# Second feed-forward product of a two-layer encoder: from plain row blocks to four phases, eight of 11 row pairs by seven products of quarters

## The chip, the cores and the metric

One NeuronCore of a Trainium2 chip runs the whole program. The metric is the device time of one execution in microseconds; three runs of the kernel before give 1254.53, 1255.04 and 1256.59 us, median 1255.04. One further execution was profiled, and every row below is from it.

## What is computed

Two layers over x of 512 tokens by 1024, float32. Each layer has four mixers and then the feed-forward part, which the change is about:

```python
h = rmsnorm(x, ffn_norm_pre[l])
gate, up = jnp.split(h @ ffn_w_in[l], 2, axis=-1)
f = (jax.nn.silu(gate) * up) @ ffn_w_out[l]
x = x + rmsnorm(f, ffn_norm_post[l])
```

`ffn_w_in` is 1024 x 5632 and `ffn_w_out` 2816 x 1024. The first line's product is called the first product here, the one with `ffn_w_out` the second. The output is x after the second layer.

## The kernel before, in words

**Numbers.** Every float32 factor is split in two: `hi` is the value rounded to fp32r by ScalarE (ACT), `lo` is the rest, by VectorE (DVE) or GpSimd (POOL). `mm3` multiplies by three passes of TensorE (PE), hi x hi, hi x lo and lo x hi.

**Order of the work.** The program is written by a planner at build time (`Builder.go`). Threads are Python generators that yield the engine of their next piece ("P", "A", "V", "G" for POOL, "D" for the SP queue) or a condition. `Timed` prices each instruction, `LAT` each handover, and `go` always takes the piece that can start earliest, ties by priority. The order on each engine is fixed by that; on the chip semaphores alone decide when each instruction starts. Plain loads are issued on SP (`dma`, L383), loads that add to a tile on POOL (`add_load`, L504; `sums` is the DVE part). Tokens stand for memory: 74 tiles "m" of 128x512 float32, 4 pairs "w" for split weights, 8 PSUM banks (3 "d", 5 "x").

**First product** (`ffn_in`). Three of the 22 blocks of gate and up are done plainly (`parts`), 19 by Strassen's seven products of quarters (`prod`, 256 columns wide). Their results are kept unsplit; 19 threads `f_conv` split them after the first product has ended (`self.conv`), and `ffn_act` does so at once for the first three.

**Second product** (`ffn_out`). For each 512-column half of the output and each of the 22 row blocks k, one weight block of 128x512 is split (`w_split`, on DVE or POOL) and four token blocks t are multiplied with it, 12 matmuls of 512 columns:

```python
for half in range(2):
    for k in range(KF):
        w = yield from self.w_get()
        for t in range(NT):
            self.mm3(b[half][t], (f[k][0][:, ts], f[k][1][:, ts]), w, k == 0, k == KF - 1)
```

In the second half the last eight row blocks are held back (`TAIL`) and done token block by token block, 24 matmuls each, so that the norm of block t (`chain`: square, `rstd` with a power on POOL, update of x, and the next layer's `pre_norm` with its transposes on PE) runs beside the matmuls of block t + 1. The next layer's first product starts on tokens 0 to 255 as soon as two blocks are normalised (`CUTS`). After layer 2, `put` stores x.

## Time and profile before

| | us |
|---|---|
| median of three runs | 1255.04 |
| the profiled execution | 1254.46 |
| its span | 1252.7 |
| second product, layer 1 | 505.4 to 625 |
| second product, layer 2 | 1125.8 to 1246.2 |

The span is from the first to the last instruction; 1.8 us of the execution lie around it. Engines are busy at the same time, so their times do not add up. PEld is PE's weight load, which overlaps its matmuls. In the chain, a piece is the work that released the next one. A line number L191 is that of a helper through which nearly all instructions are issued, so instructions are told apart by their tiles: `wh` and `wl` are hi and lo of a weight, `m` any tile, `bd` and `bx` PSUM banks, `in_wf` the feed-forward weights in memory.

### The profile page before, as it was taken

Reading aid. Unit: us, or ns where it says so; the run is one execution under the profiler, and the core shown is the slowest. Engines: PE = TensorE matmul, PEld = TensorE weight load, DVE = VectorE, ACT = ScalarE, POOL = GpSimd, SP = SyncE. Lnnn points to the kernel's source line nnn. Section 1 sums busy time; section 2 is a strip of 40 time slices with the busy share of each in tenths; the row PEclk is TensorE's granted clock in tenths of the full one; section 3 lists DMA queues with packets and bytes.
Section 4 is the critical chain, followed back from the end, with each engine's and each line's share of the span. In section 5 each row is a group of like instructions: output and inputs, shape, how many; then the busy total and the mean of one; then the engine's idle time right before and its main releaser. Section 6 shows DMA issues by size and latency. Waiting matters only on the chain.

```text
span 1252.7 us, 21225 instructions
## 1 busy us (share of the span) xinstructions
PE 1218.5 (97%) x7906; PEld 1067.7 (85%) x7906; DVE 783.7 (63%) x1602; ACT 658.2 (53%) x1448; POOL 232.6 (19%) x216
## 2 busy tenths in 40 slices
PE   7999999999999999999989899999999999999997
PEld 6876777789999999888887677677899999998886
DVE  6467674589667777612554766655897677765232
ACT  6476754565455555523438647445655455554330
POOL 5021111132111111212230111112411211102120
PEclk9999999999999999999989899999999999999999
DMA  6523125117776562325451221260386865532331
GB/s 216 196 89 97 48 60 179 68 62 178 172 189 179 149 152 77 116 87 167 155 195 51 68 85 35 77 204 24 91 192 164 196 165 147 144 99 96 102 117 68
DMA packets 77239, 155.11 MB, mean 124 GB/s; under 512 B 9040, under 2 KB 9424, under 8 KB 77136
## 3 DMA queue, kind: packets, MB, share of 16 engines
q1 hardware_dynamic: 65904, 133.31, 32.5%
q0 software_dynamic: 10944, 19.93, 9.8%
q8 instruction: 62, 1.02, 0.3%
q10 hardware_dynamic: 288, 0.52, 0.1%
q14 instruction: 41, 0.34, 0.1%
HBM read 147.44 MB, written 4.19 MB: 121 GB/s over the span
## 4 chain that ended last, share of the span: by engine, by line
PE 84%; DVE 6%; ACT 5%; issue 2%; POOL 1%; DMA 1%; SPq 0%; POOLq 0%; DVEq 0%; ACTq 0%
PE bx L191 42%; PE bd L191 41%; DVE m L191 5%; ACT m L191 4%; POOL s L191 1%; ACT L191 1%; DVE s L191 1%; DMA ws<-in_w 0%; ACT wh L191 0%; POOL wl L191 0%; POOL m L191 0%; DMA m<-in_w 0%; PE warm L191 0%; DVE wl L191 0%; DVE sbd L191 0%
## 5 line engine op out<-in xcount | busy, mean ns | idle before, releaser
L191 PE MATMUL bd<-m,wh 128*128 128x256 f32 (+1 forms) x1696 | 374.5, 315 | 1.1 <-DVE m L191 1.0
L191 DVE TENSOR_TENSOR wl<-m,wh 128x512 fp32r<-128x512 f32 x286 | 198.2, 694 | 155.1 <-ACT wh L191 145.5
L191 PEld LDWEIGHTS bd<-m,wh 128*128 128x128 f32 x1696 | 275.0, 191 | 22.6 <-issue 6.0
L191 ACT CAST wh<-m 128x512 fp32r<-128x512 f32 x318 | 196.9, 619 | 146.1 <-PE bd L191 74.2
L191 PE MATMUL bx<-m,m 128*128 128x256 f32 (+8 forms) x1736 | 255.8, 335 | 9.5 <-DVE m L191 9.0
L191 PE MATMUL bd<-m,wl 128*128 128x256 f32 (+1 forms) x848 | 264.3, 312 | 0.0
L191 PEld LDWEIGHTS bx<-m,m 128*128 128x128 f32 (+3 forms) x1736 | 195.5, 178 | 59.2 <-issue 26.0
L191 DVE TENSOR_TENSOR m<-m,m 128x512 f32<-128x512 f32 (+3 forms) x286 | 172.9, 622 | 42.0 <-ACT m L191 40.2
L191 PEld LDWEIGHTS bd<-m,wl 128*128 128x128 f32 x848 | 161.8, 191 | 9.3
L191 PE MATMUL bx<-wh,m 128*128 128x512 f32 x472 | 163.7, 392 | 0.0
L191 PE MATMUL bx<-m,wh 128*128 128x256 f32 x832 | 154.3, 283 | 0.9 <-ACT bd L191 0.9
L191 PEld LDWEIGHTS bx<-m,wh 128*128 128x128 f32 x832 | 129.8, 192 | 1.3 <-ACT bd L191 1.3
L191 PE MATMUL bd<-wh,m 128*128 128x512 f32 x360 | 128.8, 392 | 0.0
L506 POOL DMA_DIRECT2D m<-in_wf x76 | 67.1, 976 | 315.5 <-DVE m L191 87.3
L191 ACT CAST wh<-ws 128x512 fp32r<-128x512 f32 x86 | 53.3, 621 | 126.2 <-PE bd L191 76.9
L191 DVE TENSOR_TENSOR wl<-ws,wh 128x512 fp32r<-128x512 f32 x56 | 42.2, 754 | 122.5 <-ACT wh L191 122.0
L191 PE MATMUL bx<-m,wl 128*128 128x256 f32 x416 | 117.7, 283 | 0.0
L191 PEld LDWEIGHTS bx<-wh,m 128*128 128x128 f32 x472 | 89.1, 189 | 19.0 <-issue 0.5
L191 POOL TENSOR_TENSOR wl<-m,wh 128x512 fp32r<-128x512 f32 x32 | 49.1, 1535 | 286.4 <-ACT wh L191 236.1
L191 POOL TENSOR_TENSOR wl<-ws,wh 128x512 fp32r<-128x512 f32 x30 | 47.9, 1596 | 263.9 <-ACT wh L191 242.8
L191 PE MATMUL bd<-m,m 128*128 128x256 f32 (+1 forms) x624 | 92.4, 303 | 0.9 <-ACT m L191 0.9
L191 PE MATMUL bx<-wl,m 128*128 128x512 f32 x236 | 92.3, 391 | 0.0
(105 smaller groups left out, 1479.6 us busy)
## 6 DMA issues: line engine op xcount, KB each, us to landing
m<-in_wf SPq DMA_DIRECT2D x234, 256.0 KB, 3.8
m<-in_wf POOLq DMA_DIRECT2D x76, 256.0 KB, 4.9
ws<-in_wf SPq DMA_DIRECT2D x34, 512.0 KB, 3.6
m<-in_w SPq DMA_DIRECT2D x64, 256.0 KB, 4.5
ws<-in_w SPq DMA_DIRECT2D x16, 512.0 KB, 3.8
m<-in_wo SPq DMA_DIRECT2D x24, 256.0 KB, 3.8
m<-in_x SPq DMA_DIRECT2D x14, 256.0 KB, 4.8
m<-in_rpb SPq DMA_DIRECT2D x12, 256.0 KB, 5.1
```

Of the source, the lines that this page charges most:

```text
L191: return f(out, *a, **k)
L506: self.nc.gpsimd.dma_start(q[name], src, accum_op=ALU.add)
```

## The change

The 22 row blocks become 11 pairs j. A pair's activations are four quarters (tokens 0 to 255 and 256 to 511 by row block 2j and 2j + 1: A11, A12, A21, A22), its weights four blocks of 128x512 (B11, B12, B21, B22). Eight pairs use Strassen's seven products with Winograd's sums, three pairs (`std`, and D11, D21) the eight plain ones. The sums of products are collected over all pairs, so there are four phases: A collects A11 B11 in bank 1 and s5 t1 in bank 2; B adds s6 t2 in bank 3, A12 B21 in bank 1, s4 B22 in bank 2, and the three plain pairs (with bank 4); C adds s3 t3 and D adds A22 t4 in bank 3. A "bank" here is two PSUM banks, one for each 128-token block u.

The activations' sums s3 to s6 are made in place on DVE (`f_pair`), each factor is split as it is needed (`f_factor`, 256 wide). The weights' sums are made by loads that add: t1, t2 and t4 follow from B11 in one tile (`t_chain`), each added after the one before has been split; t3 is a plain load and one that adds. `w_factor` splits a weight, up to LOOK = 8 steps ahead of its use, always on DVE. Loads start up to 14 steps ahead (WAHEAD), activations are split up to seven ahead (FAHEAD). Between phases `out_joins` forms the sums of banks that the results need, and PE waits for them where a bank is used again (`before`). Tokens 0 to 255 are complete after phase B and go through `half`, `finish` and, between layers, `pre_norm` while PE is in C and D; tokens 256 to 511 after C (one column half) and D (the other), where the last two products of the phase are done token block by token block.

```diff
+WAHEAD = 14
+HKEEP = 8
+LPRI = 1.5
+LOOK = 8
+FAHEAD = 7
+KP = KF // 2
+KS = KP - 3
...
 def stream(self):
-            for h in range(2):
-                for i in range(KF // 2):
-                    yield d["wf2"][l, h, i], "m" if h and 2 * i >= KF - TAIL else "w"
+            yield l, "out"
...
+    def out_factors(self, l, n):
...
+        std = lambda j: [("B", j, "B11", ((1, "A11"),)), ("B", j, "B21", ((1, "A12"),)),
+                         ("B", j, "m12", ((2, "A11"), (4, "A21"))), ("B", j, "m22", ((2, "A12"), (4, "A22")))]
+        steps = []
+        for j in range(KS):
+            steps += [("A", j, "B11", ((1, "A11"),)), ("A", j, "t1", ((2, "s5"),))]
+        done = KS
+        for j in range(KS):
+            steps += [("B", j, "t2", ((3, "s6"),)), ("B", j, "B21", ((1, "A12"),)), ("B", j, "B22", ((2, "s4"),))]
+            while done < KP and (done - KS + 1) * KS <= (j + 1) * (KP - KS):
+                steps += std(done)
+                done += 1
+        steps += [("C", j, "t3", ((3, "s3"),)) for j in range(KS)]
+        for j in range(KS):
+            steps += [("D", j, "t4", ((3, "A22"),))]
+        for j in range(KS, KP):
+            steps += [("D", j, "D11", ((3, "A21"),)), ("D", j, "D21", ((3, "A22"),))]
...
+        for j in range(KP):
+            q = lambda h, k: w[l, h, j][:, k * 512:(k + 1) * 512]
+            if j < KS:
+                self.spawn(self.t_chain(o[j], at[j, "B11"], {x: at[j, x] for x in ("t1", "t2", "t4")},
+                                        (q(0, 0), q(1, 0), q(1, 1), q(0, 1))), 0)
+                parts = (("B21", (q(0, 1),)), ("B22", (q(1, 1),)), ("t3", (q(1, 0), q(1, 1))))
+            else:
+                parts = (("B11", (q(0, 0),)), ("B21", (q(0, 1),)), ("m12", (q(1, 0),)), ("m22", (q(1, 1),)),
+                         ("D11", (q(0, 0),)), ("D21", (q(0, 1),)))
+            for x, p in parts:
+                self.spawn(self.w_part(o[j], x, at[j, x], p), 0)
...
+    def t_chain(self, o, at, use, src):
+        yield lambda: at < self.wuse + WAHEAD and len(self.tok["m"]) >= 1 + ROOM
...
+        self.dma(t, src[0], 262144)
...
+        for more, before, name in zip(src[1:], ("B11", "t1", "t2"), ("t1", "t2", "t4")):
+            yield lambda: before + ".s" in o["n"]
+            yield from self.more_load(t, more, use[name])
+            o["n"].add(name)
...
+    def more_load(self, tile, src, use):
+        self.cur.pri = use / 1000.0 - 5.0
+        yield "G"
+        self.nc.gpsimd.dma_start(tile, src, accum_op=ALU.add)
+        self.cost += 1000.0
+        self.moved = max(self.moved, self.start + self.cost + 650.0) + 262144 / 180.0
+        self.cur.after = self.moved + 1500.0
...
+    def w_factor(self, i, o, x):
+        yield lambda: x in o["n"] and (
+            self.wnext == i and (self.tok["w"] or len(self.tok["m"]) >= 2 + FROOM)
+            or self.wnext >= self.out_at and i < self.wuse + LOOK and len(self.tok["m"]) >= 4 + FROOM)
...
+            yield from self.split(w[:2], o[x], "V")
...
+    def f_pair(self, j, f, o):
...
+        yield "V"
+        tt(a[:, hi], b[:, hi], a[:, hi], ALU.subtract)
+        n |= {"fA11", "fs5", "fA12", "fA22"}
+        yield lambda: "fA11.s" in n
...
+        tt(a[:, lo], a[:, lo], a[:, hi], ALU.add)
...
+        tt(b[:, lo], a[:, lo], b[:, lo], ALU.subtract)
...
+        tt(a[:, hi], a[:, lo], b[:, hi], ALU.subtract)
...
+    def f_factor(self, i, o, x):
+        yield lambda: (self.fnext == i and "f" + x in o["n"] and i < self.fuse + FAHEAD
+                       and len(self.tok["m"]) >= 1)
...
+        yield "A"
+        self.act.activation(t[:, 0:HALF], src, AF.Copy, scale=-1.0 if x == "s6" else 1.0)
+        yield "V"
...
+            self.dve.tensor_tensor(t[:, HALF:L], src, t[:, 0:HALF].bitcast(F32), ALU.subtract)
...
-    def f_conv(self, i, a, f):
...
 def ffn_in(self, l, h, ok, f):
+        for j in range(KP):
+            self.outs[l][j] = {"n": set()}
+            self.spawn(self.f_pair(j, f, self.outs[l][j]), 3)
...
 def ffn_act(self, i, b, f):
-        self.dve.tensor_tensor(a, a, b[1], ALU.mult)
+        self.dve.scalar_tensor_tensor(a, a, -1.0, b[1], ALU.mult, ALU.mult)
-        o = self.mr2()
-        yield from self.split(o, a)
...
+    def out_joins(self, x1, x2, x3, x4, n, g, acc, res):
+        def one(u):
...
+            yield lambda: "A" in n
+            yield "A"
+            self.act.copy(p, x1[u])
+            n.add(("p", u))
+            yield "V"
+            tt(r, p, x2[u], ALU.add)
+            n.add(("r", u))
+            yield lambda: "6" in n
+            yield "V"
+            tt(v, p, x3[u], ALU.add)
+            n.add(("v", u))
+            yield lambda: "B" in n
+            self.spawn(self.half(u, 0, x1[u], "d", g, acc[u], res), LPRI)
+            yield "V"
+            tt(v, v, x2[u], ALU.add)
+            self.give("x")
+            self.spawn(self.half(u, 1, v, None, g, acc[u], res), LPRI)
+            if KS < KP:
+                yield "V"
+                tt(r, r, x4[u], ALU.add)
+                self.give("dx"[u])
+            yield lambda: ("C", u) in n
+            yield "V"
+            tt(r, r, x3[u], ALU.add)
+            n.add(("c", u))
+            self.spawn(self.half(2 + u, 1, r, None, g, acc[2 + u], res), u - NT)
+            yield lambda: ("D", u) in n
+            yield "V"
+            tt(p, p, x3[u], ALU.add)
+            self.give("x")
+            self.spawn(self.half(2 + u, 0, p, None, g, acc[2 + u], res), u - NT)
...
 def ffn_out(self, l, g, gi, h, ok, f):
+        before = {("B", 1): "p", ("B", 2): "r", ("C", 3): "v", ("D", 3): "c"}
...
+            tail = mine[-2:] if ph in "CD" else []
...
+                for us in ((0,), (1,)) if tail and i == mine[-1][0] else ((0, 1),):
+                    for i2, dst, j2, y2, w2, wl in rest:
+                        t = held[j2, y2]
+                        for u in us:
+                            if (ph, dst) in before:
+                                yield lambda: (before[ph, dst], u) in n
+                            yield "P"
+                            self.mm3(bank[dst][u], (t[:, u * P:(u + 1) * P], t[:, HALF + u * P:HALF + (u + 1) * P]), w2,
+                                     dst in fresh, i2 == last[ph, dst], skip_group_check=True)
```

## Rows read from the trace of the kernel before

**Rows 1.** The page, busy time of the engines: us, share of the span, instructions
```profile
PE 1218.5 (97%) x7906; PEld 1067.7 (85%) x7906; DVE 783.7 (63%) x1602; ACT 658.2 (53%) x1448; POOL 232.6 (19%) x216
```

**Rows 2.** The page, chain that ended last, share by engine
```profile
PE 84%; DVE 6%; ACT 5%; issue 2%; POOL 1%; DMA 1%; SPq 0%; POOLq 0%; DVEq 0%; ACTq 0%
```

**Rows 3.** The chain in order of time, second product: start us, us, what
```profile
506.10 2.06 PE bx L191 x9
...
604.03 10.88 PE bd L191 x48
```

**Rows 4.** Stages: us; PE, PEld, DVE, ACT, POOL busy; granted clock; DMA share; GB/s
```profile
317.40:498.80 181.40, 181.40 (x1514) 181.40 (x1514) 131.63 (x232) 95.97 (x197) 26.32 (x31) 1.00 0.61 152
505.40:565.20 59.80, 59.80 (x268) 49.61 (x268) 25.17 (x38) 24.43 (x45) 12.57 (x6) 1.00 0.31 102
565.20:625.00 59.80, 59.80 (x274) 49.69 (x273) 25.18 (x50) 24.68 (x61) 13.36 (x13) 1.00 0.46 154
```

**Rows 5.** Timeline of DVE, runs back to back: start us, us, instruction, count
```profile
287.88 2.76 DVE L191 TENSOR_TENSOR m<-m 128x256 f32<-128x256 f32 x8
...
506.55 5.50 DVE L191 SCALAR_TENSOR_TENSOR m<-m,m 128x512 fp32r<-128x512 f32 x9
```

**Rows 6.** Timeline of ACT, a run back to back
```profile
505.48 3.24 ACT L191 ACTIVATE m<-m 128x512 fp32r<-128x512 f32 x6
```

**Rows 7.** The tile in_wf: ns min/median/max of each load's issue; landing of all
```profile
L384 SPq DMA_DIRECT2D m<-in_wf x234: 327/328/1524, 187.7 to 1206.1; - x117
L506 POOL DMA_DIRECT2D m<-in_wf x76: 862/875/1938, 283.5 to 1094.9; - x76
...
DMA to landing us min/median/max: 2.5/4.1/9.5
```

**Rows 8.** DMA queues, 280 to 317 us: packets, MB, share of 16 engines
```profile
q1 hardware_dynamic: 2691, 4.91, 41.4%
q0 software_dynamic: 1152, 2.10, 34.1%
```

**Rows 9.** DMA queues, 317 to 400 us
```profile
q1 hardware_dynamic: 5667, 10.30, 39.2%
q0 software_dynamic: 2350, 4.29, 32.3%
```

**Rows 10.** Adding loads, median us to landing: all, then 283.5 to 297 us
```profile
m<-in_wf POOLq DMA_DIRECT2D x76, 256.0 KB, 4.9
...
m<-in_wf POOLq DMA_DIRECT2D x5, 256.0 KB, 8.0
```

**Rows 11.** PE's waits, 495 to 506 us: us, times, longest
```profile
PE bd L191 <- DVE m L191: 0.5, 1, 0.5
```

**Rows 12.** PE's waits, 600 to 662 us
```profile
PE bx L191 <- DVE m L191: 3.1, 1, 3.1
```

**Rows 13.** Stage 630 to 645 us, columns as in rows 4
```profile
630.00:645.00 15.00, 11.85 (x78) 11.65 (x78) 11.76 (x25) 7.35 (x22) 6.32 (x8) 0.77 0.76 246
```

**Rows 14.** Timeline of PE, eight transposes at full clock
```profile
622.45 1.03 PE L191 MATMUL bx<-ident,m 128*128 128x128 f32 x8
```

**Rows 15.** The chain in order of time, after the wait of rows 12
```profile
638.78 1.97 PE bx L191 x8
640.75 2.56 PE bd L191 x12
643.31 9.29 PE bx L191 x72
652.60 8.64 PE bd L191 x72
```

**Rows 16.** Timeline, end of the last two token blocks
```profile
1240.82 0.60 ACT L191 ACTIVATE m<-bx 128x512 f32<-128x512 f32 x1 [4.75 <-PE bx L191]
...
1246.26 0.60 ACT L191 ACTIVATE m<-bx 128x512 f32<-128x512 f32 x1 [4.75 <-PE bx L191]
...
1248.47 0.74 DVE L191 SCALAR_TENSOR_TENSOR m<-m,s,m 128x512 f32<-128x512 f32 x1
```

More of the change, by code (lines that the diff above doesn't have):

```diff
@@ L446, in w_load @@
                 n += (7 if src[1] > NP else 4) + (3 if src[1] == KF - 1 else 0)
+                continue
+            if kind == "out":
+                n = self.out_factors(src, n)
                 continue
@@ new lines, in w_part @@
+    def w_part(self, o, x, at, parts):
+        yield lambda: at < self.wuse + WAHEAD and len(self.tok["m"]) >= 1 + ROOM
+        self.take("m", 1)
+        o[x] = self.m()
+        yield "D"
+        self.dma(o[x], parts[0], 262144)
+        if len(parts) > 1:
+            yield from self.more_load(o[x], parts[1], at)
+        else:
+            yield "V"
+        o["n"].add(x)
+    def more_load(self, tile, src, use):
[6 more added lines that the diff above has]
+        yield "V"
+        self.cost = 0.0
@@ new lines, in w_factor @@
+    def w_factor(self, i, o, x):
+        yield lambda: x in o["n"] and (
+            self.wnext == i and (self.tok["w"] or len(self.tok["m"]) >= 2 + FROOM)
+            or self.wnext >= self.out_at and i < self.wuse + LOOK and len(self.tok["m"]) >= 4 + FROOM)
+        early = self.wnext != i
+        self.taken.add(i)
+        while self.wnext in self.taken:
+            self.taken.remove(self.wnext)
+            self.wnext += 1
+        if self.tok["w"] and not early:
+            self.take("w")
+            w = (self.whp.tile([P, 512], F32R, tag="wh", name=self.nm("wh")),
+                 self.wlp.tile([P, 512], F32R, tag="wl", name=self.nm("wl")), "w", 1)
+        else:
+            self.take("m", 2)
+            w = (*self.mr2(), "m", 2)
+        if x[0] == "m":
+            yield "A"
+            self.act.activation(w[0], o[x], AF.Copy, scale=-1.0)
+            yield "V"
+            self.dve.scalar_tensor_tensor(w[1], o[x], -1.0, w[0].bitcast(F32), ALU.mult, ALU.subtract)
+        else:
+            yield from self.split(w[:2], o[x], "V")
+        o["n"].add(x + ".s")
+        if "t4" not in o or x in ("B21", "B22", "t3", "t4"):
+            self.give("m")
+        self.wrdy[i] = w
@@ L1513, in pair_sums @@
         self.give("d")
-        self.spawn(self.f_conv(i, a, f), 4)
-    def f_conv(self, i, a, f):
-        yield lambda: self.conv
-        yield from self.need(2, 0)
-        o = self.mr2()
-        yield "A"
-        self.act.activation(o[0], a, AF.Copy, scale=-1.0)
-        yield "V"
-        self.dve.scalar_tensor_tensor(o[1], a, -1.0, o[0].bitcast(F32), ALU.mult, ALU.subtract)
-        self.give("m")
-        f[i] = o
+        f[i] = a
     def ffn_in(self, l, h, ok, f):
@@ L1557, in ffn_in @@
                     who[4].add(n)
+                    if i + (who is new) >= KF:
+                        self.give("m", 4)
             old = new
-        self.conv = True
-        self.give("m", 28)
     def ffn_act(self, i, b, f):
-        yield from self.need(3, 0)
+        yield from self.need(1, 0)
         a = self.m()
@@ new lines, in ffn_act, with half, finish @@
+        f[i] = a
+    def half(self, t, i, y, bank, g, acc, res):
+        yield from self.square(acc, i, y)
+        yield "V"
+        j = self.att[t // 2][t % 2] if bank else y
+        if i == 0:
+            self.dve.scalar_tensor_tensor(j, y, -1.0, g[i], ALU.mult, ALU.mult)
+        else:
+            self.dve.tensor_tensor(j, y, g[i], ALU.mult)
+        if bank:
+            self.give(bank)
+        res[t, i] = j, not bank
+        if (t, 1 - i) in res:
+            res[t] = 1
+    def finish(self, t, gi, h, ok, acc, res):
+        yield lambda: t in res
+        r = yield from self.rstd(acc)
+        for i in range(2):
+            xs = self.x[t][i]
+            yield "V"
+            self.dve.scalar_tensor_tensor(xs, res[t, i][0], r, xs, ALU.mult, ALU.add)
+            if res[t, i][1]:
+                self.give("m")
+            if h is None:
+                self.spawn(self.put(t, i, xs), t - NT)
+        if h is not None:
+            yield lambda: "h" in res
+            yield from self.pre_norm(t, gi, h, ok, False)
@@ L1629, in dense @@
             f = {}
+            self.fnext, self.fuse = 0, 0
             yield from self.ffn_in(l, h, ok, f)
```

161 lines of the change are left out of this document (120 added, 41 removed).

## The prediction

> **What bounds the kernel now.** I read the page's table of busy time first. TensorE (PE) is busy for 1218.5 us, 97% of the span, VectorE (DVE) for 783.7 [rows 1]. A busy PE is not proof, so the chain that ended last comes next: PE holds 84% of it [rows 2]. In order of time the chain shows the second feed-forward product as an unbroken string of matmuls, nine in 2.06 us at its start and 48 in 10.88 us near its end, 226.7 ns each [rows 3]. The table by stage confirms it: in both halves of the product PE is busy for 59.8 of 59.8 us at full clock, while DVE works 25.2 us and the DMA engines 0.31 and 0.46 of the time [rows 4]. So in this stage time is matmuls counted, and there is room on every other engine. The first product (the first line of the same table) matters because it is already done by Strassen's seven products: its PE is busy for 181.4 of 181.4 us with DVE at 73% and the DMA engines at 0.61. That is the nearest evidence that such a scheme can feed PE.
>
> **The matmuls removed.** A quarter product is 6 matmuls of 512 columns (two token blocks, three passes), 6 x 226.7 ns = 1.36 us. A row pair takes 8 now and 7 by Strassen. Per layer that is 48 x 11 = 528 matmuls now and 42 x 8 + 48 x 3 = 480 after: 48 fewer, 10.88 us by the row of 48; over two layers **-21.76 us**, all on the path. Their shape does not change, so neither does their price.
>
> **Work on DVE and ScalarE (ACT).** Back to back, DVE gives a 512-wide instruction every 0.603 us ((5.50 - 0.68)/8) and a 256-wide one every 0.335 us [rows 5]; ACT a 512-wide one every 0.524 us ((3.24 - 0.62)/5, one alone lasting 0.62) [rows 6]. Per layer there are 8 x 7 + 3 x 6 = 74 weight factors to split (512 wide) and 8 x 7 + 3 x 4 = 68 activation factors (256 wide), each once on ACT and once on DVE; 32 sums of activations, 256 wide; 12 joins and 8 gain products, 512 wide, all on DVE. DVE: 74 x 0.603 + 68 x 0.335 + 32 x 0.335 + 20 x 0.603 = 90.2 us in 480 x 0.2267 = 108.8 us, 83% (now 42%). ACT: 142 x 0.524 = 74.4 us if its narrow instructions cost as much as the wide, and under 10 for squares and copies: 78% at most. The 19 conversions of `f_conv` and the three of `ffn_act` go. I cost all of this at nothing: PE covers it, as it covers 73% in the first product. If the cover were gone (PE waiting on something else) it would matter by phase: phase A asks per pair for 2 x 0.603 + 3 x 0.335 = 2.2 of 2.72 us, and phase C, with its joins and gain products, for 12.3 in 10.9 us. Up to eight weight factors and seven activation factors may be prepared ahead, 10.9 us of PE, so I expect C to live on stock.
>
> **Transfers.** SP: 50 plain loads a layer at 0.33 us each are 16.5 us of issue, no bound. POOL: 4 adding loads per Strassen pair, 32 a layer at 0.88 us, 28 us of issue [rows 7]; POOL's low halves in this stage go, and DVE's sum above holds them. On the engines, from 280 to 317 us the plain queue moved 4.91 MB (18.7 loads) in 41.4% of 37 us, 0.82 us a load, and the adding queue 2.10 MB (8 loads) in 34.1%, 1.58 us a load [rows 8]. Check: the first product's 5 plain and 2 adding loads per 10.08 us ask for 72%, and the engines show 39.2 + 32.3 = 71.5% [rows 9]. A Strassen pair now asks for 4 x 0.82 + 4 x 1.58 = 9.6 us against 9.52 us of PE; a plain pair for 4.9 against 10.9. Per layer 91.5 of 108.8 us: it fits, but phase A does not. There t1 and the next link, t2, are both released per pair: 0.82 + 2 x 1.58 = 4.0 us against 2.72 us, with phase B's plain loads beside it.
>
> **The chain in phase A** decides the size of the gain. t1 is B11 with another quarter added in place, so it needs: B11 split (1.4 us: 0.62 on ACT, 0.68 on DVE, a handover), an adding load, t1 split (1.4 us). B11 may be split eight steps before its own use, so 10.9 us are there. Issue to landing of an adding load has a median of 4.9 us, 8.0 us in a burst of them [rows 10], and 9.5 us is the longest of any weight load [rows 7]: chains of 7.7, 10.8 and 12.3 us. The first costs nothing, the last 1.4 us in every eight steps, 2.8 us for A's sixteen. With the queue asked for more than it can give I take the long row: 2.8 us a layer, **+5.6 us**. Bounds: 0, and everything in one line, 15 adding and 10 plain loads, 31.9 us, begun some three products (4.3 us) ahead of A: the last t1 is split at 29.0 us where it is due at 20.4, 8.6 us a layer, 17.2 in all.
> The Trainium skill (DMA: Bandwidth & Descriptors, section on the anatomy of one DMA on the gpsimd path) fits a load as 2.0 us plus bytes over 436 GB/s, an estimated 2.6 us here, and by that the chain would be 5.4 us and the sum 5.6 us lower; the trace's loads that add take longer than this fit, so I don't use it.
>
> **New waits of PE.** At A's end PE's third product waits for bank 1 copied and its fourth for a sum on DVE; they come 1.4 and 2.7 us later, about what ACT and DVE need. At C's end D's second token block waits one DVE instruction, 0.6 us and a handover, with three matmuls, 0.68 us, to cover it. Today's same kind of wait, PE on DVE at the end of the first product, is 0.5 us [rows 11]. I take 0.8 us a layer, **+1.6 us** (0 to 4). ACT's and DVE's next splits queue behind these; the stock covers that.
>
> **The layer's edge.** Today PE waits 3.1 us for the last token block's norm [rows 12], and the granted clock of 630 to 645 us is 0.77, a part of it at 1.2 instead of 2.4 GHz [rows 13]: eight transposes take 1.97 us, 1.03 us a little earlier [rows 14], and 12 matmuls 2.56 us where 1.44 would do at the 120 ns of the 72 in 8.64 us further on [rows 15]. That gap costs 3.1 + 2.7 = 5.8 us, the 0.65 us over in the 72 after it included. After the change two token blocks are normalised under C and D, so the next layer's first half starts at once; but the last two blocks' chains get longer and PE's order is fixed by the same planner with the same misjudgement. I take **0** (-5.8 to +3).
>
> **The end.** After the last matmul come a square, the power, two updates and the store [rows 16]. Now a join of 0.6 us and a handover go in front and the two last blocks follow each other by 1.4 us instead of 5.4, so their updates share DVE: **+1.0 us** (0.7 to 2.4).
>
> **Sum.** The profiled execution took 1254.46 us (span 1252.7; the median of the runs is 0.6 us higher). 1254.46 - 21.76 + 5.6 + 1.6 + 0 + 1.0 = **1240.9 us**, a 1.1% gain. With A's chain fully hidden and the edge's gap closed it would be 1229.5; with A's upper bound 1252.5.
>
> **Rivals.**
> *All hidden, and the edge closes*: 1229 to 1234 us. For it: the first product shows no wait, and today's gap stands exactly where the new order puts work. Against: the landings of [rows 10]. Chance 0.13.
> *The adding queue sets phase A's pace*: 5 to 8.6 us a layer, and where a wait grows to the 3 us of [rows 12] the clock falls for a few us more: 1246 to 1256 us, 1250 in the middle. For it: 4.0 us asked in 2.72. Against: t2 isn't due until B and B11 is loaded early. Chance 0.19.
> *POOL's queue blocks itself*: slower. POOL issues in program order, and the planner prices an adding load at 4.6 us (1.0 + 0.65 + 1.46 + 1.5 in the code). A t2 waiting at the head for its t1's split holds up the t1s behind it, for up to 4.9 + 1.4 = 6.3 us each time. Gain and other costs balance at (21.76 - 2.6)/2 = 9.6 us a layer, so it decides from two such holds a layer: 1254.46 - 21.76 + 4 x 6.3 + 2.6 = 1260.5 us. For it: real landings are later than priced [rows 10]. Against: in the first product the same queue waits for splits too, and PE is never idle [rows 4]. Chance 0.08.
> *The clock falls in phase A*: short waits between short bursts might keep PE at its lower level. The sixteen products would take twice 21.8 us: 1254.46 - 21.76 + 43.5 + 2.6 = 1278.8 us. The trace has half clock after the 3.1 us wait and full clock through the waits of 0.5 us. Chance 0.02.
> The Trainium skill (TensorE: Matmul & The Clock Gate, section on HAM oscillation) tells of such a loop, where waits for loads make every burst start slow; by that rule this rival's price holds, and the trace agrees only for the long wait.
>
> **How the numbers follow.** The forecast, 1234 to 1247 us, has 0.58. A measurement of this kernel can tell 0.2%, 2.5 us. Faster by more: 0.58 + 0.13 + three quarters of 0.19 = 0.85; within: 0.05; slower: 0.10. The range of 1231 to 1252 leaves out both slower rivals, the top of the queue's case and the best of the first, some 0.2.
>
> **What would show it.** Right: 226.7 ns per matmul with 480 a layer in the second product, a stage of 109 to 114 us instead of 119.7, DVE near 83% in it, the DMA engines near 0.9 in phase A, and PE's waits in it on a DVE split with an adding load before it. Wrong: unbroken matmuls in phase A (chain hidden); waits of 3 us or a granted clock under 1.0 in it; a POOL queue idle on a split while later t1 loads are due; waits in phase C on DVE (stock not built). The prediction falls if the matmuls' price changes or the stage isn't bound by PE at all.

## The result, and the profile after

The changed kernel takes **1245.9 us** (median of four runs, 1244.61 to 1246.83) where the kernel before takes 1254.88 on the same chip: a ratio of 0.9926, 95% interval 0.9912 to 0.9940. So it is faster by 9.0 us where 13.6 were forecast. The profiled execution took 1245.09 us, its span is 1243.3 us.

The page of the changed kernel: busy time, the chain that ended last, the two large DMA queues.

```profile
PE 1203.1 (97%) x7810; PEld 1050.1 (84%) x7810; DVE 883.8 (71%) x1867; ACT 707.5 (57%) x1604; POOL 246.7 (20%) x255
...
q1 hardware_dynamic: 72672, 136.46, 34.6%
q0 software_dynamic: 20160, 36.71, 17.8%
...
PE 76%; issue 7%; DVE 7%; DMA 4%; ACT 4%; POOL 2%; SPq 0%; POOLq 0%; DVEq 0%; ACTq 0%
```

Beside [rows 1, 2]: 96 matmuls fewer, 15 us less of busy PE, 100 us more of DVE, and the chain now spends 76% of the span on PE, not 84%. Which stages those detours are in, the table by stage shows: phase A of layer 1, phases B and C, phase D, the stage of [rows 13], and phase A of layer 2.

```profile
507.96:532.92 24.96, 23.26 (x98) 17.82 (x97) 21.22 (x45) 17.22 (x39) 12.33 (x15) 1.00 1.10 242
532.92:600.00 67.08, 67.08 (x297) 55.57 (x296) 52.75 (x111) 42.92 (x100) 12.03 (x14) 1.00 0.80 201
600.00:622.00 22.00, 21.90 (x105) 17.92 (x103) 17.66 (x43) 12.72 (x38) 5.20 (x7) 1.00 0.49 159
...
630.00:645.00 15.00, 13.00 (x95) 12.49 (x94) 10.78 (x27) 7.17 (x25) 4.38 (x7) 0.89 0.86 294
...
1121.30:1147.00 25.70, 23.79 (x98) 17.77 (x98) 21.19 (x45) 16.78 (x38) 12.45 (x15) 1.00 1.09 239
```

Phases B to D run as the first product did in [rows 4]: PE without a gap but for 0.4 us at the turn to D, though DVE is at 79% in B and C. Phase A alone is loose. It holds 96 matmuls, 21.76 us, and takes 24.96 and 25.70. The matmuls' price stands (chain in order of time, phase B, 226.7 ns each):

```profile
535.81 2.72 PE bx L198 x12
```

To set the two kernels beside each other I cut the span at four places in PE's timeline, in each layer: the first 256-wide matmul of the feed-forward part, the first 512-wide one (the second product begins), the last 512-wide one, and the next layer's first 256-wide one of that part (all of layer 2's mixing lies in that last stretch, the edge between the layers with it). Lengths in us, worked out from those starts (the second product with its last matmul, 0.23 us, which the last row holds as well in layer 2):

| stretch | before | after | difference |
|---|---|---|---|
| start to layer 1's feed-forward part | 284.78 | 285.31 | +0.53 |
| first product, layers 1 and 2 | 221.15, 221.15 | 222.65, 222.65 | +3.00 |
| second product, layers 1 and 2 | 121.48, 119.70 | 114.26, 113.17 | -13.75 |
| edge and mixing of layer 2 | 277.80 | 276.49 | -1.31 |
| last matmul's start to the end | 6.85 | 9.00 | +2.15 |
| span | 1252.7 | 1243.3 | -9.4 |

The first row says nothing of the change. Up to there PE does the same instructions in the same order in the kernel before, the changed kernel and every run below, and the stretch takes 284.2 to 287.5 us in their profiled executions. The mixing of layer 2, at the end of the fourth row, spreads too (227.3 to 229.3 us), so half a microsecond of that row is no finding either.

Four detours have to be explained: phase A, the end of the first product, the edge, the tail.

**Phase A.** PE's waits, 507 to 535 us (us, times, longest):

```profile
PE bx L198 <- DVE wl L198: 1.1, 3, 0.5
PE bx L198 <- ACT wh L198: 0.6, 2, 0.5
```

The DMA queues of the changed kernel, 500 to 530 us (packets, MB, share of 16 engines), and its weight loads (KB, median us to landing):

```profile
q0 software_dynamic: 2017, 3.69, 68.9%
q1 hardware_dynamic: 1812, 3.32, 34.2%
...
m<-in_wf POOLq DMA_DIRECT2D x17, 256.0 KB, 8.9
m<-in_wf SPq DMA_DIRECT2D x12, 256.0 KB, 7.2
```

PE waits for the split of a weight (`wl` and `wh` are its halves), each time in front of a t1 of the last pairs: the starts of its matmuls show gaps from 523.7 us on, the largest 0.74 (the view, which counts from the modelled end of a matmul, has 1.7 of the 3.2 us). Split late means landed late: 8.9 us against 4.9 in [rows 10]. The queues' shares add up to 103% of the engines.

**The first product.** The chain in order of time near its end (start us, us, what):

```profile
480.74 0.76 DVE m L198 x2
481.50 0.60 DVE wl L198
482.10 0.35 DVE m L198
482.44 0.39 ACT m L198
482.83 0.02 issue
482.86 0.44 DVE bd L198
483.30 0.04 issue
483.34 1.69 PE bd L198 x12
```

DVE's timeline at the same place:

```profile
481.08 0.42 DVE L198 TENSOR_TENSOR m<-m,m 128x256 fp32r<-128x256 f32 x1
481.41 0.69 DVE L198 TENSOR_TENSOR wl<-m,wh 128x512 fp32r<-128x512 f32 x1
482.01 0.76 DVE L198 TENSOR_TENSOR m<-m 128x256 f32<-128x256 f32 x2
482.86 0.43 DVE L198 TENSOR_TENSOR bd<-bd,m 128x256 f32<-128x256 f32 x1
```

The sum in the bank `bd` at 482.86 is one of the first product's own, and PE stands for it: one wait of 1.36 us by the matmuls' starts, at the same place in both layers and absent before. Ahead of it in DVE's order stand 256-wide instructions that touch no bank, a split (481.08) and two sums (482.01): by their shapes the new work on the activations. But they are over by 482.77, and the sum in the bank starts 0.03 us after the copy that it reads, which ACT ends at 482.83. So it is this copy that is late, and not for DVE's time. Copies from a bank to a tile or another bank in ACT's timeline:

```profile
462.02 0.36 ACT L198 COPY bd<-bx 128x256 f32<-128x256 f32 x1 [0.94 <-PE bx L198]
464.90 0.37 ACT L198 COPY m<-bx 128x256 f32<-128x256 f32 x1 [0.94 <-PE bx L198]
472.10 0.36 ACT L198 COPY bd<-bx 128x256 f32<-128x256 f32 x1 [0.62 <-PE bx L198]
482.17 0.36 ACT L198 COPY bd<-bx 128x256 f32<-128x256 f32 x1 [0.94 <-PE bx L198]
482.44 0.38 ACT L198 COPY m<-bx 128x256 f32<-128x256 f32 x1
```

Each block of the first product has two of them, one into a bank and 2.9 us later one into a tile. For the block that begins with 472.10 the second comes at 482.44, 7.5 us late, behind the first copy of the next block. In the code (`pair_first`) it asks for two free tiles "m" first. The plan, which is made at build time by the code shown, has none free for it at this block and the next in the changed kernel, e1, e5 and e8, which all show the wait, and three or more in the kernel before, e3, e6, e10 and e12, which do not. What e3, e6, e10 and e12 hold back are the sums and splits of activations; each split made ahead takes a tile. (The free tiles are read from the plans; no trace shows them.)

**The edge and the tail.** PE's one wait from 600 to 640 us:

```profile
PE bx L198 <- DVE m L198: 1.9, 1, 1.9
```

The transposes behind it, in PE's timeline:

```profile
634.37 3.53 PE L198 MATMUL bx<-ident,m 128*128 128x128 f32 x16 [1.91 <-DVE m L198]
```

The timeline of DVE, ACT and POOL behind the last matmul, which begins at 1234.3 us:

```profile
1234.74 0.69 DVE L198 TENSOR_TENSOR m<-m,bx 128x512 f32<-128x512 f32 x1 [0.67 <-PE bx L198]
1235.35 0.69 DVE L198 SCALAR_TENSOR_TENSOR m<-m,m 128x512 f32<-128x512 f32 x1
1235.46 0.63 ACT L198 ACTIVATE m<-m 128x512 f32<-128x512 f32 x1 [0.64 <-DVE m L198]
...
1236.22 0.69 DVE L198 SCALAR_TENSOR_TENSOR m<-m,m 128x512 f32<-128x512 f32 x1
...
1236.84 0.74 DVE L198 SCALAR_TENSOR_TENSOR m<-m,s,m 128x512 f32<-128x512 f32 x1
...
1237.73 0.99 POOL L198 TENSOR_TENSOR s<-s,mhalf 128x1 f32<-128x1 f32 x1 [0.99 <-DVE s L198]
1238.75 1.42 DVE L198 SCALAR_TENSOR_TENSOR m<-m,s,m 128x512 f32<-128x512 f32 x2 [0.44 <-POOL s L198]
```

The wait of [rows 12] is down from 3.1 to 1.9 us, and the granted clock of 630 to 645 us is 0.89 where it was 0.77 [rows 13]. In the tail a join (1234.74) and two gain products stand where a square followed the last matmul in [rows 16], and both blocks' updates queue on DVE.

### The profile page after: what moved, and what is told of

Same layout as the page of the kernel before. It is cut to its first block, busy times and chain, and to the rows that moved or that the text cites. A ratio compares the mean times of both kernels' runs of the same rounds, so it can differ in the third digit from the quotient of the medians.

```text
span 1243.3 us, 21744 instructions
## 1 busy us (share of the span) xinstructions
PE 1203.1 (97%) x7810; PEld 1050.1 (84%) x7810; DVE 883.8 (71%) x1867; ACT 707.5 (57%) x1604; POOL 246.7 (20%) x255
## 4 chain that ended last, share of the span: by engine, by line
PE 76%; issue 7%; DVE 7%; DMA 4%; ACT 4%; POOL 2%; SPq 0%; POOLq 0%; DVEq 0%; ACTq 0%
PE bx L198 40%; PE bd L198 36%; DVE m L198 5%; ACT m L198 3%; DMA m<-in_wf 3%; POOL wl L198 1%; DMA ws<-in_w 1%; ACT wh L198 1%; DVE wl L198 1%; POOL s L198 1%; POOL m L601 0%; DVE s L198 0%; DMA m<-in_w 0%; POOL att L289 0%; DVE sbd L198 0%
## 5 line engine op out<-in xcount | busy, mean ns | idle before, releaser
L198 PE MATMUL bx<-m,m 128*128 128x256 f32 (+8 forms) x2096 | 334.0, 340 | 9.7 <-DVE m L198 9.0
L198 DVE TENSOR_TENSOR m<-m,m 128x512 fp32r<-128x512 f32 (+3 forms) x551 | 297.1, 571 | 39.5 <-ACT m L198 37.3
L198 PEld LDWEIGHTS bx<-m,m 128*128 128x128 f32 (+2 forms) x2096 | 257.1, 180 | 70.6 <-issue 25.6
L198 ACT ACTIVATE m<-m 128x256 fp32r<-128x256 f32 (+1 forms) x246 | 112.2, 482 | 61.5 <-DVE m L198 54.9
L514 POOL DMA_DIRECT2D m<-in_wf x76 | 66.9, 973 | 306.2 <-DVE m L198 121.4
L198 PEld LDWEIGHTS bd<-m,m 128*128 128x128 f32 x864 | 119.5, 191 | 8.9 <-DVE m L198 1.4
L198 ACT CAST m<-m 128x512 fp32r<-128x512 f32 x184 | 108.0, 614 | 15.2 <-DVE m L198 12.7
L198 PE MATMUL bx<-wh,m 128*128 128x512 f32 x296 | 105.7, 398 | 1.6 <-ACT wh L198 1.4
L601 POOL DMA_DIRECT2D m<-in_wf x64 | 56.1, 964 | 165.6 <-DVE m L198 115.2
L198 PE MATMUL bd<-wh,m 128*128 128x512 f32 x232 | 80.7, 394 | 0.0
L198 PEld LDWEIGHTS bx<-m,wl 128*128 128x128 f32 x384 | 73.8, 192 | 0.0
```

The source lines that it names most:

```text
L198: return f(out, *a, **k)
L514: self.nc.gpsimd.dma_start(q[name], src, accum_op=ALU.add)
L601: self.nc.gpsimd.dma_start(tile, src, accum_op=ALU.add)
```

## The experiments

Every run is a version of the changed kernel. All ratios are against the kernel before on the same chip in the same series (its medians: 1254.06 to 1256.18); the lengths are those of the table above, in two columns layer 1 and layer 2. In question for phase A was whether the adding queue sets its pace, or the splits on ACT and DVE.

| run | us | ratio [95%] | first product | second product | edge, mixing | tail |
|---|---|---|---|---|---|---|
| the change | 1245.9 | 0.9926 [0.9912, 0.9940] | 222.65, 222.65 | 114.26, 113.17 | 276.49 | 9.00 |
| e1_no_add | 1240.09 | 0.9873 [0.9858, 0.9889] | 222.67, 222.67 | 111.06, 110.29 | 275.57 | 9.60 |
| e2_t2_later | 1251.94 | 0.9971 [0.9954, 0.9987] | 222.67, 222.66 | 114.18, 111.71 | 283.63 | 8.96 |
| e3_late_sums | 1256.14 | 1.0007 [0.9996, 1.0018] | 223.38, 222.63 | 115.18, 117.17 | 280.23 | 9.36 |
| e4_tail4 | 1247.58 | 0.9934 [0.9918, 0.9950] | 222.67, 222.66 | 114.36, 112.85 | 280.05 | 8.20 |
| e5_b11_first | 1239.38 | 0.9869 [0.9846, 0.9892] | 222.82, 222.81 | 111.12, 109.33 | 276.38 | 9.02 |
| e6_release1 | 1245.78 | 0.9918 [0.9894, 0.9941] | 221.20, 221.21 | 116.28, 115.30 | 275.61 | 8.92 |
| e7_edge | 1245.03 | 0.9910 [0.9887, 0.9933] | 222.67, 222.66 | 114.29, 112.78 | 275.95 | 8.83 |
| e8_k11 | 1245.26 | 0.9919 [0.9891, 0.9946] | 222.97, 222.96 | 114.39, 110.77 | 277.00 | 10.01 |
| e9_first_k11 | 1240.45 | 0.9881 [0.9858, 0.9904] | 222.97, 222.97 | 110.63, 109.00 | 275.52 | 10.06 |
| e10_first_release | 1239.08 | 0.9877 [0.9849, 0.9905] | 221.21, 221.48 | 113.54, 110.47 | 275.71 | 8.87 |
| e11_first_release_tail | 1237.64 | 0.9862 [0.9839, 0.9884] | 221.21, 221.48 | 113.38, 110.35 | 276.62 | 8.15 |
| e12_together | 1235.53 | 0.9853 [0.9826, 0.9880] | 221.21, 221.20 | 111.16, 109.41 | 277.24 | 8.38 |

**e1_no_add: what the adding costs.** The second load of t1 to t4 overwrites instead of adding; the weights' sums are left out.

```diff
-        self.nc.gpsimd.dma_start(tile, src, accum_op=ALU.add)
+        self.nc.gpsimd.dma_start(tile, src)
```


> The links of the second product's weight chains are loaded from POOL's queue as plain loads over the tile instead of adding to it; this leaves out the weights' sums t1, t2, t3 and t4 and keeps every issue, split and wait. In the changed kernel phase A's sixteen products take 24.96 and 25.70 us in the two layers where 21.77 would do, with waits that grow over the last four pairs. Theory 1, the DMA engines are asked for more than they give in A because an adding load takes 1.58 us of them and a plain one 0.82: demand in A falls from 4.0 to 2.5 us per pair of 2.72 us, A takes under 22.5 us in both layers, the DMA share in A falls well below the 1.10 seen, and the time falls by 5 to 7 us to about 1239. Theory 2, the chain's length itself (split, issue, landing, split) is what is late, whatever the engines do: landings get shorter by 1 us or so, A stays over 23.5 us, the time falls by less than 3 us. Theory 3, DVE's or ACT's order in A is late: A stays at 25 us and the time at 1245.

Measured: phase A runs without a gap in layer 1 and loses some 1.1 us in layer 2; the second product is 3.2 and 2.9 us shorter. The table by stage, the queues and landings (500 to 530 us) of this run:

```profile
508.00:533.00 25.00, 24.53 (x113) 20.30 (x112) 23.01 (x49) 18.88 (x43) 8.22 (x16) 1.00 0.86 287
```
```profile
q0 software_dynamic: 1359, 4.46, 44.1%
...
m<-in_wf POOLq DMA_DIRECT2D x17, 256.0 KB, 4.5
```

(The 0.5 us missing from PE lies at the seam of the two products, ahead of A.) More bytes, 4.46 MB, take a smaller share, and a load lands in 4.5 us, not 8.9. DVE does more than in the changed kernel's A, so DVE's volume is not what A waits for. One thing did not change: how long POOL stands at the head of its queue for a split. POOL's waits from 507 to 530 us, first in the changed kernel, then in this run:

```profile
POOL m L601 <- DVE wl L198: 6.9, 4, 2.7
```
```profile
POOL m L601 <- DVE wl L198: 6.9, 5, 2.9
```

The same 6.9 us, and here they cost PE nothing. So POOL's holds alone are not the cause; they cost only together with late landings.

**e2_t2_later: t2 out of the way.** The load that makes t2 waits until t2 is within eight steps of its use.

```diff
-            yield lambda: before + ".s" in o["n"]
+            yield lambda: before + ".s" in o["n"] and (name != "t2" or use[name] < self.wuse + 8)
```


> The second link t2 of each chain is held back until its use is within eight weight steps, so three of its loads instead of seven compete with the t1 loads in phase A. Theory 1 (DMA engines over-asked in A): the t1 loads land earlier, A falls from 24.96 and 25.70 us to under 23 us, the time falls by 3 to 6 us to 1240 to 1243, unless t2 or t4 is now late in phase B, which would show as waits of PE there (none now). Theory 2 (chain length): A and the time stay as they are, within 1 us. Theory 3 (order on DVE or ACT): the same as theory 2.

Measured: phase A has no gap left but 0.4 us at its turn to B in layer 1; yet the time rises to 1251.9. Waits come back later, early in B of layer 2 (1.36 us at 1155) and at the turn from C to D, as in PE's timeline of this run:

```profile
602.43 0.94 PE L198 MATMUL bx<-m,m 128*128 128x512 f32 x3 [1.76 <-DVE m L198]
603.88 2.32 PE L198 MATMUL bx<-m,m 128*128 128x512 f32 x9 [0.51 <-DVE m L198]
```

The rest, 7.1 us, is the edge: waits of 4.2 and 4.1 us in all, where the changed kernel has one of 1.9. The planner orders the edge anew whenever anything ahead of it changes, so a whole time says little about phase A; its own length does.

**e3_late_sums: the sums kept out of the first product.** The sums and splits of activations are released when the first product is over.

```diff
-        yield lambda: 2 * j in f and 2 * j + 1 in f
+        yield lambda: self.over and 2 * j in f and 2 * j + 1 in f
```


> The activations' sums and splits for the second product (f_pair, and so f_factor) start only after the first product has ended; one part of the change undone. The first product's end, from the start of its Strassen part to the first 512-wide matmul of the second product, takes 189.98 us in the changed kernel and 188.54 before, with one wait of 1.2 us of PE on a sum of DVE that stands behind the new activation sums and splits. Theory: the wait is made by this early work; it goes, the stretch falls to 188.5 us plus what phase A's start now waits for its first activations, 0.5 to 2 us, so the time stays within 2 us of 1245.9. Rival: the wait comes from the weight splits that run ahead or from planning anew, and stays at 1.2 us; then the time rises by 1 to 2 us for the later start.

Measured: the wait of 1.36 us in the first product is gone in both layers, so the early sums and splits were its cause; by the copies above, through the tiles that they take and not through DVE's time. It is paid back with interest: the stretch is no shorter, since PE stands for the first split activations at its end (2.0 and 1.3 us), A now begins without stock (gaps of up to 1.9 us in layer 1 and 4.5 us in layer 2), and the whole is no faster than the kernel before.

**e4_tail4: a longer tail.** The last four products of D, not two, go block by block, so that the first block is done earlier.

```diff
-            tail = mine[-2:] if ph in "CD" else []
+            tail = mine[-4:] if ph == "D" else mine[-2:] if ph == "C" else []
```


> The last four products of phase D, instead of the last two, are done token block by token block, so the last two blocks end 2.7 us apart instead of 1.4. In the changed kernel 8.6 us pass from the last matmul to the end of the span, 6.45 before. Theory: the two blocks' closing instructions stand in each other's way on DVE and POOL (the last power waits for an update of the other block); the 8.6 us fall to about 7.3, which is the old tail and one join of 0.8 us, and the time falls by 1 to 1.5 us. Rival: the tail is longer only because of the join, square and gain product that now come in a row; it stays at 8.4 us or more and the time is the same within 0.5 us.

Measured: the tail is 0.8 us shorter. The whole is not: the same edit moves the edge, +3.6 us (waits of 2.8 and 2.4 us there).

**e5_b11_first: the same work in another order.** All eight B11 products of phase A come first, then the eight with t1. Not a load, a sum or a matmul is saved.

```diff
-            steps += [("A", j, "B11", ((1, "A11"),)), ("A", j, "t1", ((2, "s5"),))]
+            steps += [("A", j, "B11", ((1, "A11"),))]
+        for j in range(KS):
+            steps += [("A", j, "t1", ((2, "s5"),))]
```


> Phase A takes all eight products with B11 first and then the eight with t1, so that every t1 load can be asked for before the t2 loads and has eight more products of time. What the engines must move in all is unchanged. Theory 1a, A is late because t2 loads that are not yet due stand ahead of t1 loads in the adding queue: phase A's loss (3.2 and 3.9 us of PE in the changed kernel's two layers) falls under 1 us in both, and the second product gets 2.5 to 3.5 us shorter in each layer, from 114.3 and 113.2 us. Theory 1b, it is the sum of what A asks of the engines: the loss only moves, to the end of A or the start of B, and the second product's length changes by less than 1 us. The whole time follows the second product, 1240 to 1241 or 1245 to 1246, if the edge between the layers stays as it is (1.9 us of wait); in earlier runs it did not when the planner planned anew, so the product's length is the measure.

Measured: 1239.38 us, and phase A without any gap in both layers. The table by stage, the queues and the landings (500 to 530 us) of this run:

```profile
508.00:533.00 25.00, 25.00 (x112) 20.71 (x111) 18.90 (x41) 14.45 (x33) 11.30 (x13) 1.00 1.10 250
```
```profile
q0 software_dynamic: 1881, 3.44, 64.3%
q1 hardware_dynamic: 1828, 3.35, 36.7%
...
m<-in_wf POOLq DMA_DIRECT2D x19, 256.0 KB, 12.8
```

The DMA engines are as full as in the changed kernel (1.10 in both), the median landing is even 3.9 us longer, and PE never waits. By the weights that POOL's loads fetch, its order in the changed kernel is t1 of pairs 0 to 3, t2 of 0, t1 of 4, t2 of 1, t1 of 5, t2 of 2 and 3, t1 of 6, t2 of 4, t1 of 7; here it is the eight t1, then the eight t2, then t4. So in the changed kernel t1 loads that were due stood behind t2 loads that nobody needs before B. The adding loads land in this order, one after another: here the first sixteen from 507.6 to 537.9 us, 2.0 us apart on average. The t1 of pair 7 is the 13th of them in the changed kernel; it lands at 529.9 us and is used at 530.7, where 528.4 would be its time without a wait. Here it is the eighth, lands at 520.8 and is used at 528.2.

This run alone does not part order from lead: B11's product now stands eight products ahead of t1's, not one, so there can be up to 9.5 us more between asking for a t1 and using it. e2 parts them. It leaves the products as they are, its POOL queue too has all eight t1 ahead of the first t2, the t1 of pair 7 lands at 527.3 for a use at 530.7, and A is clean in both layers. With e1 this says that the loss needs both: the price of adding, and t2 in front of t1. Whether a t2 in front costs more by its transfer or by its hold at POOL's head is not parted: in e2 POOL waits for no split of a `wl` from 507 to 530 us, in e5 for 4.8 us, 1.2 at the longest.

**e6_release1: half way between the change and e3.** Sums and splits are released at the last pair of the first product.

```diff
+            if i >= KF - 1:
+                self.over = True
```


> The activations' sums and splits for the second product may start when the first product reaches its last pair, instead of as soon as memory is free. Theory: the wait of 1.36 us in the first product disappears as in the run that released them after the first product, and phase A's first factors are ready in time, so the stretch from the feed-forward part's first matmul to the second product's first falls from 222.65 to 221.2 us, the length before the change, in both layers; phase A's own loss may grow, since DVE has less done ahead (3.2 and 3.9 us now; over 4 us if that matters). Rival: a new wait appears at the last pair in its place, and the stretch stays at 222.6.

Measured: the first product's wait is gone (221.20 us), and the second product is 2.0 and 2.1 us longer, with waits like this one (PE's waits, 1110 to 1150 us):

```profile
PE bx L198 <- ACT wh L198: 2.9, 2, 2.4
```

No net gain: the 1.4 us moved by one stage. In layer 2 they are in phase A, whose loss rises from 3.9 to 6.1 us; in layer 1 A stays at 3.3 and the gaps are at the turn to D and before transposes in D.

**e7_edge: the last two blocks' transposes planned 3.5 us later.**

```diff
+        if gi != V_GM and not keep and t >= 2:
+            self.cur.after = max(self.cur.after, self.start + self.cost + 3500.0)
```


> At the edge between the layers the transposes of the last two token blocks are planned 3.5 us later, behind 12 more matmuls of the next layer's first half, which need nothing of them; nothing else is changed. Theory: PE's order there is fixed by a planner that takes the norm's chain for shorter than it is; with the later place the wait of 1.9 us falls under 0.6 us, the lower clock that follows it goes, and the stretch from the second product's end in layer 1 to the feed-forward part of layer 2 falls from 276.5 us by 2.5 to 4 us; the time falls to about 1242.5. Rival: the chain is late by its own length and the transposes are waited for whenever they come; the stretch stays within 1 us.

Measured: a miss. The wait of 1.91 us falls to 0.46 and the clock stays up behind it, but another of 1.1 us comes 4 us later (PE's waits, 505 to 670 us), and the stretch is only 0.5 us shorter:

```profile
PE bx L198 <- ACT m L198: 1.1, 1, 1.1
```

**e8_k11: all 11 pairs by seven products**, 462 matmuls a layer, 18 fewer (-4.1 us a layer at 226.7 ns).

```diff
-KS = KP - 3
+KS = KP
```


> All 11 row pairs by seven products, no plain pairs. PE has 18 matmuls, 4.1 us, fewer in each layer's second product: 462 of them, 104.7 us without loss against 108.8. Theory 1: the engines are asked for 11 x 9.6 = 106 us, more than PE's own time, and phase A's loss goes on growing by 0.7 to 1 us for each further pair; the loss in the second product rises from 3.6 and 4.1 us to 6 to 10 us, and the product's length gains under 2 us a layer or loses. Rival (chain length or order only): the loss stays about 4 us and the second product falls by 4 us a layer, to 110 and 109 us.

Measured: no difference to the change in the whole. The second product has 0.1 us more in layer 1 and 2.4 less in layer 2, and the tail has 1.0 more. A loses no more than with eight pairs (3.1 and 3.7 us), so theory 1 is wrong there. What is new are gaps late in C, at the turn to D and in D (in layer 1 7.8 us in all against 3.6). In C, DVE is busy all the time; phase C of layer 1 in the changed kernel, then in this run:

```profile
590.04:600.92 10.88, 10.88 (x49) 9.01 (x48) 10.51 (x22) 9.25 (x24) 0.00 (x0) 1.00 0.67 191
```
```profile
586.29:602.97 16.68, 15.74 (x68) 11.95 (x66) 16.68 (x35) 15.16 (x37) 1.64 (x3) 1.00 0.89 224
```

PE waits there for a `wl` and at the turn for a sum, both of DVE. So with eight pairs C just fits, 10.51 us of DVE in 10.88, and with 11 the stock no longer carries it: it is DVE that takes the gain here, not the adding loads.

**e9_first_k11: e5 and e8 together.** Their two diffs.

> Phase A takes all products with B11 first, and all 11 row pairs go by seven products. With B11 first alone the second product's loss was 0.6 and 0.4 us; with 11 pairs alone 7.8 and 5.8 us. Theory: most of the loss with 11 pairs is t2 standing ahead of t1 as well, but the engines' sum (106 us asked in 104.7) must now show later: loss of 2 to 4 us a layer, the second product at 107 to 109 us against 111.1 and 109.3, the time at 1235 to 1239. Rival: the sum decides, loss stays at 5 us or more, and the time is 1241 or over.

Measured: 1240.45, no better than e5. A is clean; the gaps are in C and at the turn to D (4.0 and 4.2 us), with DVE busy for all of the 16.98 us of C in layer 1. They take most of the 4.1 us saved: the second products are 0.5 and 0.3 us shorter than e5's, and the tail is 1.0 longer.

**e10_first_release: e5 and e6 together.** Their two diffs.

> Phase A takes all products with B11 first, and the activations' sums and splits start at the first product's last pair. The release alone took the wait of 1.36 us out of the first product and put it back as loss in phase A, at its third and fourth product, where t1 and s5 came late. Theory: with B11 first these come eight products later, so nothing is paid back; the stretch before the second product is 221.2 us and the second product stays at 111.1 and 109.3 us, the time is 2.5 to 3.2 us below the 1239.4 of B11 first alone. Rival: DVE lacks the work that it had done ahead, whatever the order; the second product's loss rises by over 1 us a layer and the time stays at 1239.

Measured: the first product is 1.6 and 1.3 us shorter than in e5, the second 2.4 and 1.1 longer (a wait of 1.51 us early in B): given back again, later.

**e11_first_release_tail: e10 with e4's tail in the last layer alone**, where no edge follows.

```diff
+            tail = mine[-4:] if ph == "D" and h is None else mine[-2:] if ph in "CD" else []
```


> As the run with B11 first and the later release, with the last four products of the last layer's phase D done token block by token block. Theory: the time from the last matmul to the end falls by 0.8 us, as when this was done alone, and the rest stays; 0.5 to 1 us below that run. Rival: nothing, or a loss on the way into phase D's end as large.

Measured: the tail is 0.7 us shorter than e10's, 8.15 us; the whole by 1.4, with intervals that overlap.

**e12_together: the shortest time.** e5's order, the release one pair earlier than in e6, e11's tail, e7's edge.

```diff
+            if i >= KF - 2:
+                self.over = True
```


> Together: phase A with B11 first, the activations' sums and splits released one pair earlier than before (at the last pair but one), the last layer's tail of four products, and the later place of the transposes at the layers' edge. Theory: released at the last pair the work came 1.5 us and 0.7 us late at the start of phase B; ten microseconds earlier it is in time, and does not yet stand in the way of the first product's sums; the stretch before the second product is 221.2 us, the second product 111 and 109.5 us, the tail 0.8 us shorter, the time 1234 to 1236. Rival: the wait in the first product comes back with the earlier release (222.7 us), and the time is 1237 to 1239, as without any release.

Measured: 1235.53 us against 1254.06 beside it, faster than both kernels; its interval overlaps those of e5, e10 and e11, so by the whole time it is not shown to be faster than these. PE has no wait from 508 to 535 us, and from 470 to 507 us this one, that of [rows 11]:

```profile
PE bd L198 <- DVE m L198: 0.5, 1, 0.5
```

The first product is back at 221.2 us, and the second stays at e5's length: released two pairs before the end, the sums come late enough for the first product and early enough for A and B.

## Why the prediction was right, and where it was wrong

The mechanism held: time in the second product is matmuls counted, at the same 226.7 ns, and its lengths of 114.26 and 113.17 us are at the upper end of the 109 to 114 forecast. Term by term, against the span:

| term | forecast | measured |
|---|---|---|
| matmuls removed | -21.76 | -21.76: 96 fewer, 226.7 ns |
| chain in phase A | +5.6 | +7.1: 3.2 and 3.9 |
| seams | +1.6 | +0.9, what is left of the second product's -13.75 |
| DVE and ACT "at nothing" | 0 | +3.0, in the first product |
| the layer's edge | 0 | -1.3 |
| the end | +1.0 | +2.15 |
| start | not in the sum | +0.5, inside the spread of the same instructions |
| sum | -13.6 | -9.4 |

**Phase A: right in place, its size in part luck.** PE does wait on splits of t1 whose adding loads land late, as the chain said. But the term was 1.4 us in every eight products, from the longest landing of 9.5 us. What came is nothing in eleven products and then 3.2 and 3.9 us at the t1 of pairs 5 to 7; and with the median measured, 8.9 us, the same chain gives 1.4 + 8.9 + 1.4 - 10.9 = 0.8 us in eight products, 1.6 a layer, less than half. What made the loss is the line: adding loads that land one after another, with five t2 ahead of the last t1. The forecast had such a line as its upper bound, with all 15 adding and 10 plain loads in it, and in the rival in which the adding queue sets A's pace. That rival had the mechanism, but its 5 us a layer were not reached. The reason given for the long row, a queue asked for more than it gives, was incomplete: in e5 the engines are as full (1.10, where I had forecast 0.9) and it costs nothing. What counts is whose load stands first. The Trainium skill (DMA: Bandwidth & Descriptors, section on the anatomy of one DMA on the gpsimd path) would by its fit have had a load land in an estimated 2.6 us; the runs differ, with 4.5 us for plain and 8.9 for adding loads in this stage.

**The step that failed** is "I cost all of this at nothing: PE covers it". The volume was right: DVE was busy for 21.22 + 52.75 + 17.66 of 114.04 us, 80% against 83 forecast, and phases B to D show no cost of it beyond the seam. But I asked for the cover only inside the second product, and only as a share of busy time. The first sums and splits are released earlier, at the end of the first product, and the splits take tiles there. A copy of the first product that needs two tiles comes 7.5 us late, and one sum in a bank and PE with it: 1.36 us of PE, in each layer (e3, e6 and e12 take it away). I had counted the engines' time of these instructions and not the memory that they hold. In phase C the share was no safe measure either: with eight pairs DVE has 0.4 us to spare there, with 11 (e8, e9) PE waits.

**The tail was mis-sized**: +2.15 within its bounds of 0.7 to 2.4. Both blocks' updates do share DVE, as the step said, but two gain products stand there as well. **The edge** was taken at no change; its row gave 1.3 us (1.8 up to the mixing, 0.5 lost in the mixing, inside its spread). e2 to e4 show that it could have cost 2 to 6 us as well. The bounds held, the reason ("the same misjudgement") is too simple: the misjudgement changes with every plan.

**The rivals.** *All hidden*: phase A was not hidden. *POOL's queue blocks itself*: the holds are there, as the forecast had it among its signs of being wrong, 6.9 us in all and 2.7 at the longest, but e1 has the same ones and loses nothing in layer 1, so alone they don't decide. *The clock falls in phase A*: the granted clock is 1.00 in both A stages through waits of up to 0.74 us. The Trainium skill (TensorE: Matmul & The Clock Gate, section on HAM oscillation) tells of a loop of waits and slow bursts; in this phase the trace shows none.

**Open** are why the planner's edge comes out so differently from plan to plan, where e7's second wait comes from, and what share of phase A's loss is a t2's hold at POOL's head and what its transfer.

## What to carry to other kernels

When an in-order queue feeds a phase, list its order before cutting its volume: loads that aren't due belong behind those that are, and an order of the products that lets the due chains go first was worth more here (e5, 7.0 us in the two second products) than fewer matmuls (e8, 2.3 there). Work that "lies under" a busy engine still takes memory from the moment when it is released: look at who else needs free tiles then, also in the stage before. And find the instruction that a late one really waited for: what stands ahead of it in its queue may be over before that. Where a planner re-orders the rest after each edit, judge an edit by the length of its own stage, and know how far that length spreads when nothing in it has changed.

## What the runs showed of the hardware that I had not expected

The DMA share of a stage can pass 1: 1.10 in phase A, where the queues' shares are 68.9% and 34.2% from 500 to 530 us. So the times of two queues overlap on an engine, and a sum of shares near 1 is not yet a wait: e5 has none. An adding load took 3.69 MB in 68.9%, a plain one on the same queue 4.46 MB in 44.1%: per byte 1.9 times the time, and its issue on POOL 0.86 us instead of 0.54. Sixteen adding loads in a row landed 2.0 us apart on average (e5): the first eight were issued within 7.1 us and landed within 13.3.

The clock fell at the edge after a wait of 1.9 us (16 transposes in 3.53 us, where 8 take 1.03 in [rows 14]), but not after the 0.46 and 1.1 us that e7 has there. In the second product it stayed at 1.00 behind waits of 1.7 (e3, at 525.5 us) and 1.76 us (e2, at 602.4), and the granted clock was 0.64 in the 4.3 us behind one of 2.4 (e6, at 1138.6) and 0.51, nearly all at 1.2 of 2.4 GHz, in the 6.3 us behind one of 4.4 (e3, at 1144.6).
